# A hybrid encoder on one core: an order of products for each pass, and head products placed side by side in the array

## The chip, the cores and the metric

The kernel runs on one core of one Trainium2 chip. The metric is the device time of one execution, in microseconds; before the change it is 3675.07 us, the median of three runs from 3674.42 to 3675.59. TensorE is called PE (its weight loads PEld), VectorE DVE, ScalarE ACT, GpSimd POOL and SyncE SP.

## The reference

Two layers run over 1024 tokens of 1024 channels. A layer normalises its input, projects it with one wide matrix, runs four token mixers on parts of the projection, gates and projects each mixer's output, adds the four, projects once more and adds the input:

```python
h = _rmsnorm(x, norm_w)
p = h @ w_in
...
u_a = _rwkv7_branch(rw_r, rw_k, rw_v, rw_wlo, rw_alo, rw_z, ...)
u_b = _retention_branch(rt_q, rt_k, rt_v, rt_z, ret_norm_w)
u_c = _ssd_branch(sd_xbc, sd_z, sd_dt, ...)
u_d = _gdn_branch(gd_qkv, gd_z, gd_b, gd_a, ...)
gates = jax.nn.sigmoid(gate_logits.reshape(b, s, N_BRANCH, D_MODEL))
merged = gates[:, :, 0] * (u_a @ w_branch[0])
...
return x + merged @ w_out
```

Retention has 8 heads with 32 channels in q and k and 64 in v; q and k are rotated by a position angle first. RWKV has 8 heads of 64 channels. All is float32. The retention scores, their decay and the state are:

```python
scores = jnp.einsum('bnihk,bnjhk->bnhij', qc, kc) * decay
y_intra = jnp.einsum('bnhij,bnjhv->bnihv', scores, vc)
k_tail = kc * jnp.exp(g_last - g)[..., None]
chunk_state = jnp.einsum('bnjhk,bnjhv->nbhkv', k_tail, vc)
```

## The kernel before

The tokens are cut in two halves of 512, so the program makes four passes: layer 0 on both halves, then layer 1. A pass works on four chunks of 128 tokens.

Most of PE's work is large products: 128 output channels by 512 tokens, summed over 1024 input channels. For float32 accuracy each operand is split in a high and a low part (wh and wl for weights, hH and hL for the normalised input), and three of the four cross products are made, so one such product is 24 matmuls of 128x512. `slab_gemm` (L649) does this; `wide_gemm` (L685) makes the token-major form, in pieces of 128x256; `narrow_gemm` (L669) makes 48 rows of decays. The result stands in one of three PSUM banks called g until DVE or ACT has evacuated it. In the first pass over a layer's weights (passes 0 and 2) ACT casts the high part, DVE subtracts the low part, and both are stored for the second pass (1 and 3), which loads them. SP's queue issues these loads and stores, a fixed number of weight slabs ahead of the product.

The mixers are twelve units a pass: two of retention (four heads each), four of gated delta, two of SSD and four of RWKV (two heads each). Each has a front (scores, triangular inverses) and a back (the state, chunk after chunk), with small products in four PSUM banks called m and one called y. In RWKV's front, `rw_front` (L1501), the low-rank decay and rate are made by two pairs of products (L1514 on), then each chunk's scores for one head after the other: three cross products for each of two operands, 64 rows high, 256 columns wide. In retention's front, `ret_front` (L1724), q is multiplied by four head masks, so that one product of 128 rows by 512 columns gives the scores of four heads; the back (L1768) makes one 128x256 product for the state, masks it, and adds it. `ev_rope` (L884) swaps the two halves of q or k by two copies on ACT.

What sets the order: `FIRST` and `PLAN` (L53, L64) are lists of large products, written by hand, for pass 0 and for the passes after it; an item `in.6.B` is input B of unit 6, `sm` the decays, `merge.ret.3` a gate and a projection, `out.2` an output projection of the pass before, and `norm` starts the normalisation of the next pass. Between the pieces of these products, `mixers` (L1281) puts steps of the mixers: it keeps a reckoning of each engine's time, and a step whose inputs it thinks ready goes next, unless DVE is thought to be more than `LEAD` microseconds behind PE. Each engine then executes its own instructions strictly in the order in which the program was written out.

At the start of the program up to four products run on the input before it is normalised (`h_gemm`, L974; the operands rH and rL lie in tiles called u) and are scaled afterwards. At the end of a pass `norm` makes hH and hL for the next one, which it can do only when the last product that reads the old ones is done.

Of the kernel before, what the change touches and what calls it, by code (L numbers as in the profile page):

```python
# [51 lines left out]

FIRST = items("""  # L53
sm in.0.k in.0.q in.0.v in.0.z0 in.0.z1 in.1.k in.1.q in.1.v in.1.z0 in.1.z1 in.2.v in.2.k in.2.q in.2.z in.3.v
in.3.k in.3.q lora in.3.z in.4.v in.4.k in.4.q merge.ret.0 merge.ret.1 merge.ret.2 merge.ret.3 merge.ret.4 in.4.z
in.5.v in.5.k in.5.q merge.ret.5 in.5.z in.6.x0 in.6.B in.6.C in.6.x1 merge.ret.6 merge.ret.7 in.6.z in.7.x0
in.7.B in.7.C in.7.x1 merge.gdn.0 merge.gdn.1 merge.gdn.2 in.7.z in.8.v in.8.k in.8.r in.8.z in.9.v in.9.k in.9.r
in.9.z merge.gdn.3 merge.gdn.4 in.10.v in.10.k in.10.r merge.gdn.5 merge.gdn.6 merge.gdn.7 merge.ssd.0 in.10.z
merge.ssd.1 in.11.v in.11.k in.11.r merge.ssd.2 merge.ssd.3 merge.ssd.4 in.11.z merge.ssd.5 merge.ssd.6
merge.ssd.7 gate.0 gate.1 gate.2 gate.3 gate.4 gate.5 gate.6 gate.7 norm proj.0 proj.1 proj.2 proj.3 proj.4 proj.5  # L60
proj.6 proj.7
""")

PLAN = items("""  # L64
in.0.k in.0.q in.0.v in.0.z0 in.0.z1 in.1.k in.1.q in.1.v in.1.z0 out.0 sm out.1 out.2 out.3 out.4 out.5 in.1.z1
in.2.v in.2.k in.2.q in.2.z in.3.v in.3.k in.3.q in.3.z in.4.v in.4.k in.4.q out.6 out.7 lora merge.ret.0
merge.ret.1 merge.ret.2 merge.ret.3 in.4.z in.5.v in.5.k in.5.q merge.ret.4 in.5.z in.6.x0 in.6.B in.6.C in.6.x1
merge.ret.5 merge.ret.6 merge.ret.7 in.6.z in.7.x0 in.7.B in.7.C in.7.x1 merge.gdn.0 merge.gdn.1 in.7.z in.8.v
in.8.k in.8.r in.8.z in.9.v in.9.k in.9.r in.9.z merge.gdn.2 merge.gdn.3 in.10.v in.10.k in.10.r merge.gdn.4
merge.gdn.5 merge.gdn.6 merge.gdn.7 merge.ssd.0 in.10.z merge.ssd.1 in.11.v in.11.k in.11.r merge.ssd.2  # L70
merge.ssd.3 merge.ssd.4 in.11.z merge.ssd.5 merge.ssd.6 merge.ssd.7 gate.0 gate.1 gate.2 gate.3 gate.4 gate.5
gate.6 gate.7 norm proj.0 proj.1 proj.2 proj.3 proj.4 proj.5 proj.6 proj.7
""")


def block_cols(kind, idx, role):
    a = np.arange(P)
    if kind == "rw":
        base = {"r": 0, "k": 512, "v": 1024, "z": 1664}[role]
        return base + P * idx + a  # L80
    if kind == "gdn":
        base = {"q": 5256, "k": 5256 + 512, "v": 5256 + 1024, "z": 6792}[role]
        return base + P * idx + a
    if kind == "ret":
        if role in "qk":
            base = 2176 if role == "q" else 2432
            x, h, i = a // 64, (a % 64) // 16, a % 16
# [26 lines left out]
SLABS = [sl for it in PLAN for sl in slabs_of(it)]  # L114
# [4 lines left out]
def sequence(npass):  # L119

    seq = [(p - (it[0] == "out"), it) for p in range(npass) for it in (PLAN if p else FIRST)]
    return [x for x in seq if x != (npass - 1, ("norm",))] + [(npass - 1, it) for it in PLAN if it[0] == "out"]

# [99 lines left out]
def make_consts():  # L223
# [18 lines left out]
    head = (a % 64) // 16  # L242
    put("hmask", (head[:, None] == np.arange(4)[None, :]).astype(f))
# [18 lines left out]
    x = a // 64  # L262
# [8 lines left out]
class Clock:  # L271
# [89 lines left out]
    def ported(self, eng, name, ins):  # L361


        if eng == "scalar" or not ins or any(self.slot.get(x.tensor.name, ("",))[0] in ("m", "g", "y") for x in ins):
            return False
        return eng == "gpsimd" or name in ("tensor_tensor", "scalar_tensor_tensor", "tensor_copy", "copy") \
            or (name == "tensor_scalar" and int(np.prod(ins[0].shape[1:])) >= 32)
# [5 lines left out]
class Engine:  # L373
# [5 lines left out]
    def __getattr__(self, what):  # L379
        fn = getattr(self.real, what)  # L380

        def call(*a, **k):
# [42 lines left out]
class Trunk:  # L425
    LEAD = 3.0
# [44 lines left out]
    def mm(self, out, lhsT, rhs, **k):  # L471
        n, m = (int(np.prod(ap.shape[1:])) for ap in (rhs, lhsT))
# [6 lines left out]
        self.ck.op("pe", [out], [lhsT, rhs], cost)  # L479
# [1021 lines left out]
    def rw_front(self, p, j, inp, box):  # L1501
# [62 lines left out]
        for s in range(2):  # L1564
# [159 lines left out]
    def ret_front(self, p, u, inp, box):  # L1724
# [27 lines left out]
        qms = []  # L1752
        for c in range(NC + 1):
            if c < NC:
                qm = W1(1 + c % 2).rearrange("p (h t) -> p h t", h=4)
# [3 lines left out]
                qms.append(qm)  # L1759
            if c > 0:  # L1760
# [3 lines left out]
            yield  # L1764
# [3 lines left out]
    def ret_back(self, p, u, box):  # L1768
# [6 lines left out]
        yB = self.t([P, 2, 256], "yB")  # L1775
        yC = self.t([P, 2, 256], "yC")
        s16 = self.t([P, NC, 4], "s16")
        for c in range(NC):
            py = self.pm()[:, 0:256]
            self.mm(py, qd[:, c], S, start=True, stop=False, skip_group_check=True)  # L1780
            for h in range(4):
                self.mm(py[:, 64 * h:64 * h + 64], A[:, c, h], va[c // 2][:, c % 2, 64 * h:64 * h + 64],
                                 start=False, stop=(h == 3), skip_group_check=True)
            pst = self.pm()[:, 0:256]
# [312 lines left out]
```

## Time and profile before

| | |
|---|---|
| median of three runs | 3675.07 us |
| the profiled execution's own time | 3677.53 us |
| its span, first to last instruction | 3675.8 us |
| mean granted TensorE clock | 0.981 |
| PE busy | 3535.3 us, 24904 matmuls |
| DVE busy | 2296.0 us |
| ACT busy | 1178.1 us |
| DMA moved | 654.21 MB, mean 178 GB/s |

In the rows of the profile `g<-hL,wh` is an instruction that writes a tile named g from tiles named hL and wh; `128*128 128x512` is the part of the array that it uses, then the size of the moving operand; `x8` is how many there are. A matmul in float32 leaves two records, one whose operands are split beforehand leaves one. A matmul's duration includes its way through the array, so steps are read from start to start. All instructions of DVE, ACT and POOL go through a recording helper and have its line, L400; matmuls have L480, transposes L484. In a row of stretches the columns are the stretch, its length, busy time and count of PE, PEld, DVE, ACT and POOL, the granted clock, the DMA share and GB/s.

### The profile page before, as it was taken

What the parts mean: (1) busy time and instruction counts of PE and PEld (TensorE: products, weight loads), DVE (VectorE), ACT (ScalarE), POOL (GpSimd) and SP (SyncE); (2) the same over time, 40 slices, a digit from 0 to 9 for tenths busy, and PEclk for the clock granted to TensorE, in tenths of its full rate; (3) what the DMA queues carried; (4) which work ended last, traced back from release to release, by engine and by line L of the source; (5) the groups of instructions that cost most, each with busy time, mean ns of one, the idle gap of its engine ahead of it and who ended that gap; (6) DMA issues with size and microseconds to landing.
All of it is one profiled execution on the core that took longest, in us unless ns stands there. A gap on an engine that the chain in (4) does not pass through costs nothing.

```text
span 3675.8 us, 66687 instructions
## 1 busy us (share of the span) xinstructions
PE 3535.3 (96%) x24904; PEld 2855.0 (78%) x24904; DVE 2296.0 (62%) x6038; ACT 1178.1 (32%) x2714; POOL 572.1 (16%) x905
## 2 busy tenths in 40 slices
PE   8998999999999999999999989999999999999998
PEld 6776887777787888777777777877778788877777
DVE  5676767677356655466547676667764666564653
ACT  4333344333132223232224333433331322232221
POOL 2101012221110111122110101122211011112220
PEclk9998999999999999999999999999999999999999
DMA  6573565656665545444676556655566544544356
GB/s 236 174 232 130 196 211 190 200 165 208 210 211 160 150 133 146 134 111 128 199 252 226 185 187 200 208 185 172 185 215 225 177 152 144 149 132 132 104 153 214
DMA packets 359171, 654.21 MB, mean 178 GB/s; under 512 B 39872, under 2 KB 43328, under 8 KB 358848
## 3 DMA queue, kind: packets, MB, share of 16 engines
q1 hardware_dynamic: 347184, 629.92, 54.3%
q10 hardware_dynamic: 11664, 20.02, 1.6%
q8 instruction: 197, 3.23, 0.4%
q14 instruction: 126, 1.03, 0.1%
HBM read 400.23 MB, written 249.56 MB: 177 GB/s over the span
## 4 chain that ended last, share of the span: by engine, by line
PE 83%; DVE 10%; DMA 2%; ACT 2%; issue 1%; POOL 1%; SPq 0%; DVEq 0%; ACTq 0%; POOLq 0%
PE g L480 60%; PE m L480 17%; PE m L484 3%; PE y L480 3%; DVE invw L400 2%; DVE w L400 1%; DMA ws<-wh 1%; DVE wl L400 1%; DVE in L400 1%; DVE cvy L400 1%; DVE yB L400 1%; POOL rs L400 1%; DVE hL L400 0%; ACT w L400 0%; DVE GD L400 0%
## 5 line engine op out<-in xcount | busy, mean ns | idle before, releaser
L480 PE MATMUL g<-hH,wh 128*128 128x512 f32 x2600 | 1075.8, 414 | 0.0
L480 PE MATMUL g<-hL,wh 128*128 128x512 f32 x2600 | 1034.8, 398 | 16.0 <-DVE hL L400 15.9
L480 PE MATMUL g<-hH,wl 128*128 128x512 f32 x2576 | 745.7, 406 | 0.0
L480 PEld LDWEIGHTS g<-hL,wh 128*128 128x128 f32 x2600 | 492.3, 189 | 128.4 <-DVE hL L400 19.3
L480 PEld LDWEIGHTS g<-hH,wh 128*128 128x128 f32 x2600 | 492.0, 189 | 117.5 <-issue 7.1
L480 PEld LDWEIGHTS g<-hH,wl 128*128 128x128 f32 x2576 | 475.7, 190 | 112.1 <-issue 8.1
L480 PE MATMUL g<-u,wh 128*128 128x512 f32 (+1 forms) x1328 | 409.0, 412 | 18.8 <-DVE u L400 11.8
L400 DVE TENSOR_TENSOR wl<-raw,wh 128x512 fp32r<-128x512 f32 x456 | 331.1, 731 | 61.3 <-ACT wh L400 40.3
L400 ACT CAST wh<-raw 128x512 fp32r<-128x512 f32 x447 | 275.2, 619 | 252.5 <-DMA ws<-wh 106.8
L480 PEld LDWEIGHTS g<-u,wh 128*128 128x128 f32 (+1 forms) x1328 | 245.0, 190 | 81.5 <-DVE u L400 18.0
L400 POOL TENSOR_TENSOR rs<-rs,mhalf 128x4 f32<-128x4 f32 (+2 forms) x80 | 106.1, 1327 | 1011.3 <-DVE rs L400 980.4
L400 DVE SCALAR_TENSOR_TENSOR cvy<-cvraw,par,cvy 128x512 f32<-128x512 f32 x244 | 186.5, 764 | 76.8 <-ACT cvy L400 68.3
L480 PE MATMUL g<-u,wl 128*128 128x512 f32 x784 | 223.4, 403 | 0.0
L400 ACT COPY cvraw<-g 128x512 f32<-128x512 f32 (+1 forms) x160 | 93.5, 584 | 301.5 <-PE g L480 254.3
L480 PEld LDWEIGHTS g<-u,wl 128*128 128x128 f32 x784 | 146.3, 190 | 33.3 <-issue 0.5
L400 ACT ACTIVATE tg<-g 128x512 f32<-128x512 f32 x100 | 59.6, 596 | 267.0 <-PE g L480 258.8
L480 PE MATMUL g<-wh,hL 128*128 128x256 f32 x512 | 126.7, 285 | 6.9 <-DVE hL L400 6.9
L480 PE MATMUL g<-wh,hH 128*128 128x256 f32 x512 | 128.4, 288 | 0.0
L400 POOL TENSOR_SCALAR_AFFINE_SELECT GA<-GA 128x512 f32<-128x512 f32 x128 | 86.5, 681 | 249.8 <-ACT GA L400 215.6
L400 POOL TENSOR_TENSOR acc<-acc,tg 128x512 f32<-128x512 f32 x64 | 84.3, 1317 | 241.9 <-DVE tg L400 176.5
L400 ACT ACTIVATE in<-g 128x512 f32<-128x512 f32 x84 | 49.3, 596 | 187.5 <-PE g L480 182.0
L480 PE MATMUL m<-w,w 64*128 64x256 f32 (+1 forms) x640 | 108.3, 299 | 1.0 <-ACT w L400 1.0
(337 smaller groups left out, 5592.8 us busy)
## 6 DMA issues: line engine op xcount, KB each, us to landing
raw<-W SPq DMA_DIRECT2D x456, 256.0 KB, 3.3
ws<-wh SPq DMA_DIRECT2D x456, 256.0 KB, 3.5
ws<-wl SPq DMA_DIRECT2D x456, 256.0 KB, 3.8
wh<-ws SPq DMA_DIRECT2D x456, 256.0 KB, 2.6
wl<-ws SPq DMA_DIRECT2D x456, 256.0 KB, 3.0
w<-x ACTq DMA_DIRECT2D x32, 256.0 KB, 4.2
tg<-rope SPq DMA_DIRECT2D x16, 256.0 KB, 4.3
cvy<-rope SPq DMA_DIRECT2D x16, 256.0 KB, 4.3
```

Of the source, the lines that this page charges most:

```text
L400: return fn(*a, **k)
L480: self.nc.tensor.matmul(out, lhsT, rhs, **k)
L484: self.nc.tensor.transpose(out, in_, ident)
```

## The change

There are seven edits.

- `FIRST` and `PLAN` become `PLANS`, a list for each pass and one for the output products at the end. Within a unit the roles stand in other orders, and large products and merges are mixed otherwise.
- `LEAD` goes from 3 to 20.
- The layout of q and k in retention is head by head (32 rows a head: 16 and 16) instead of half by half, and the swap in `ev_rope` is one shuffle on DVE within 32 rows instead of two copies on ACT.
- RWKV's scores write the two heads in turn, into two banks, so that products on rows 0 to 63 and 64 to 127 follow each other.
- In the low-rank products the two of full height come first, then the two of half height, on different rows.
- Retention's scores are, for each chunk, four products of 32 rows, one for each head, into four banks; there are no masks. The evacuation is four DVE products of 512 columns, as before.
- Retention's state is four products of 32 output rows in one bank, and four updates of 32x64 in place of a masking and an update of 128x256.

```diff
-    LEAD = 3.0
+    LEAD = 20.0
...
-        nc.scalar.copy(sw[0:64], ps[64:128])
-        nc.scalar.copy(sw[64:128], ps[0:64])
+        nc.vector.stream_shuffle(sw, ps, [i ^ 16 for i in range(32)])
...
-        for i, (ps, x) in enumerate(zip((pw, pa), self.lo[l, hf])):
+        xs = list(zip((pw, pa), self.lo[l, hf]))
+        for i, (ps, x) in enumerate(xs):
+            self.mm(ps, up[:, 0, i], x, start=True, stop=False)
+        for i, (ps, x) in enumerate(xs):
             hs = slice(64 * i, 64 * i + 64)
-            self.mm(ps, up[:, 0, i], x, start=True, stop=False)
-            self.mm(ps, up[hs, 1, i], x[hs], start=False, stop=True)
+            self.mm(ps, up[hs, 1, i], x[hs], tiles=2, start=False, stop=True)
...
-                for h in range(2):
-                    hs = slice(64 * h, 64 * h + 64)
-                    pa = self.pm()
-                    for i, pt in enumerate((bp, kp)):
-                        o = pa[:, 256 * i:256 * i + 256]
-                        self.mm(o, pt[hs, 0, cg], ah[hs, c], start=True, stop=False)
-                        self.mm(o, pt[hs, 0, cg], al[hs, c], start=False, stop=False)
-                        self.mm(o, pt[hs, 1, cg], ah[hs, c], start=False, stop=True)
+                pas = [self.pm(), self.pm()]
+                for i, pt in enumerate((bp, kp)):
+                    for n, (x, y) in enumerate(((pt[:, 0], ah), (pt[:, 0], al), (pt[:, 1], ah))):
+                        for h in range(2):
+                            hs = slice(64 * h, 64 * h + 64)
+                            self.mm(pas[h][:, 256 * i:256 * i + 256], x[hs, cg], y[hs, c], tiles=2, start=n == 0,
+                                    stop=n == 2)
+                for h, pa in enumerate(pas):
...
-                for h in range(4):
-                    nc.vector.tensor_scalar(qm[:, h, :], q[:, c * C:c * C + C], self.cc("hmask")[:, h:h + 1], None,
-                                            ALU.mult)
...
-                pa = self.pm()
-                self.mm(pa, k[:, c * C - C:c * C], qms[c - 1].rearrange("p h t -> p (h t)"), start=True, stop=True)
-                nc.vector.tensor_tensor(A[:, c - 1].rearrange("p h t -> p (h t)"), pa, rd, ALU.mult)
...
+        ps = [self.pm() for h in range(4)]
+        for c in range(NC):
+            cs = slice(c * C, c * C + C)
+            for h in range(4):
+                hs = slice(32 * h, 32 * h + 32)
+                self.mm(ps[h][:, cs], k[hs, cs], q[hs, cs], tiles=4, start=True, stop=True)
+        for h in range(4):
+            nc.vector.tensor_tensor(A[:, :, h], c4(ps[h]), rd[:, h * P:h * P + P].unsqueeze(1).to_broadcast([P, NC, C]),
+                                    ALU.mult)
...
-            self.mm(pst, kt[:, c], va[c // 2][:, c % 2], start=True, stop=True)
-            tm, sq = yB[:, c % 2], yC[:, c % 2]
-            nc.vector.tensor_tensor(tm.rearrange("p (h e) -> p h e", h=4), pst.rearrange("p (h e) -> p h e", h=4),
-                                    self.cc("hmask").unsqueeze(2).to_broadcast([P, 4, 64]), ALU.mult)
-            nc.vector.scalar_tensor_tensor(S, S, self.cc("rg")[:, u:u + 1], tm, ALU.mult, ALU.add)
+            for h in range(4):
+                self.mm(pst[H[h]], kt[:, c, H[h]], va[c // 2][:, c % 2, E[h]], start=True, stop=True)
+            for h in range(4):
+                nc.vector.scalar_tensor_tensor(S[H[h], E[h]], S[H[h], E[h]], self.cc("rg")[H[h], u:u + 1], pst[H[h]],
+                                               ALU.mult, ALU.add)
```

The argument `tiles` of `mm` only divides the reckoned cost in the planner. The first items of the lists for pass 0 show the kind of change in the order:

```diff
-sm in.0.k in.0.q in.0.v in.0.z0 in.0.z1 in.1.k in.1.q in.1.v in.1.z0 in.1.z1 in.2.v in.2.k in.2.q in.2.z in.3.v
+in.0.k sm in.0.v in.0.q in.1.k in.0.z0 in.0.z1 in.1.q in.2.q in.1.v lora in.2.v in.1.z0 in.2.k in.3.v in.3.k in.3.q
```

First place: PE in the back of the first retention unit, pass 0. GD, GA, GE, GF and GR are that unit's decayed q, scores, values and decayed k; stret is its state, w the masked q and in the k of the next unit. Before:

```order
L480 MATMUL m_991<-stret_1_95,GD_1_594 128x256
L480 MATMUL m_991<-GE_1_595,GA_2_592 128x64 x4
L480 MATMUL m_997<-GE_1_595,GR_1_593 128x256
L484 MATMUL m_1015<-con_81,in_2_662 128x128 x4
L480 MATMUL m_1021<-stret_1_95,GD_1_594 128x256
L480 MATMUL m_1021<-GE_1_595,GA_2_592 128x64 x4
L480 MATMUL m_1027<-GE_1_595,GR_1_593 128x256
L480 MATMUL m_1041<-stret_1_95,GD_1_594 128x256
L480 MATMUL m_1041<-GF_1_596,GA_2_592 128x64 x4
L480 MATMUL m_1047<-GF_1_596,GR_1_593 128x256
L480 MATMUL m_1059<-w_4_1036,in_2_662 128x512
L480 MATMUL m_1062<-stret_1_95,GD_1_594 128x256
```

And after:

```order
L495 MATMUL m_768<-stret_1_95,GD_1_613 128x256
L495 MATMUL m_768<-GE_1_614,GA_2_611 128x64 x4
L495 MATMUL m_774<-GE_1_614,GR_1_612 32x64 x4
L495 MATMUL g_746<-hH_281,wl_661 128x512 x2
L495 MATMUL g_746<-hH_281,wh_676 128x512
L495 MATMUL g_746<-hL_282,wh_676 128x512
```

Before, one chunk's products follow on the other's with no large product between them; now eight large products stand between the first and the second chunk, of which the first four are shown.

Second place: PE in the backs of gated delta, pass 0. stgdn is the state, b the corrected values, invw and GE belong to the inverse of the next unit. Before:

```order
L480 MATMUL g_3864<-u_2_1087,wl_3793 128x512 x4
L480 MATMUL m_3887<-GA_4_2748,GR_3_2749 128x128
L480 MATMUL m_3887<-stgdn_1_101,GA_4_2748 128x128
L480 MATMUL y_3479<-stgdn_1_101,GA_4_2748 128x128
L480 MATMUL m_3894<-invw_2_3499,GE_3_3453 32x32 x16
L480 MATMUL m_3913<-b_10_3890,GA_4_2748 128x128
L480 MATMUL y_3479<-b_10_3890,GD_3_2750 128x128
L480 MATMUL m_3917<-invw_2_3499 32x32 x16
L480 MATMUL m_3936<-GA_4_2748,GR_3_2749 128x128
```

And after, at a back of the next unit:

```order
L495 MATMUL g_4053<-hH_281,wl_3976 128x512 x2
L495 MATMUL m_4087<-GA_4_3335,GR_3_3336 128x128
L495 MATMUL m_4087<-stgdn_1_102,GA_4_3335 128x128
L495 MATMUL y_4086<-stgdn_1_102,GA_4_3335 128x128
L495 MATMUL g_4053<-hH_281,wl_3976 128x512 x2
L495 MATMUL g_4053<-hH_281,wh_3989 128x512
L495 MATMUL g_4053<-hL_282,wh_3989 128x512
L499 MATMUL m_4104<-con_81,in_7_3684 128x128
```

Before, small products follow on small ones from here until the next large product 27 rows later; now two to six large products stand between the steps of a chunk.

Third place: PE at the end of pass 2. yC is RWKV's last normalised output, on its way to be transposed; nrs belongs to the next pass's normalisation, and the products from u are the last projections. Before:

```order
L480 MATMUL g_28912<-hL_18952,wh_28819 128x512
L484 MATMUL m_29006<-con_81,yC_28829 128x128 x2
L480 MATMUL g_28912<-hH_18951,wl_28855 128x512 x4
L484 MATMUL m_29018<-con_81,nrs_28988 128x128 x4
L480 MATMUL g_29058<-u_8_25952,wh_28866 128x512 x8
```

And after:

```order
L495 MATMUL y_28297<-sa_29037,GA_25_28298 128x64 x2
L495 MATMUL m_29061<-con_81,w_48_28613 128x1 x4
L499 MATMUL m_29069<-con_81,yC_28911 128x128 x2
L499 MATMUL m_29074<-con_81,nrs_29066 128x128 x4
L495 MATMUL g_29114<-u_8_25749,wh_28757 128x512 x8
```

Before, sixteen large products stood between the last product from RWKV's state (`y`) and the projections, twelve of them ahead of these rows and the four with wl within them; now none does.

More of the change, by code (lines that the diff above doesn't have):

```diff
@@ L72 @@
-gate.6 gate.7 norm proj.0 proj.1 proj.2 proj.3 proj.4 proj.5 proj.6 proj.7
-""")
+PLANS = [items(text) for text in ("""
+in.0.k sm in.0.v in.0.q in.1.k in.0.z0 in.0.z1 in.1.q in.2.q in.1.v lora in.2.v in.1.z0 in.2.k in.3.v in.3.k in.3.q
+in.2.z in.1.z1 in.4.k in.3.z in.4.v merge.ret.0 merge.ret.1 in.5.k in.4.q merge.ret.2 merge.ret.3 merge.ret.4 in.5.v
+in.4.z in.5.q in.6.x0 merge.ret.5 in.5.z merge.ret.6 in.6.B in.6.C in.6.x1 merge.ret.7 in.7.B in.7.x0 in.6.z in.7.x1
+merge.gdn.0 in.7.C in.8.v merge.gdn.1 merge.gdn.2 in.7.z in.8.k in.8.r in.9.v in.8.z in.9.k merge.gdn.3 in.9.r
@@ new lines @@
+merge.gdn.4 merge.gdn.5 merge.gdn.6 in.10.v in.9.z merge.gdn.7 in.10.k in.10.r merge.ssd.0 in.11.v in.10.z
+merge.ssd.1 merge.ssd.2 merge.ssd.3 merge.ssd.4 merge.ssd.5 in.11.r in.11.k merge.ssd.6 merge.ssd.7 gate.0 gate.1
+in.11.z gate.2 gate.3 gate.4 gate.5 gate.6 gate.7 proj.0 proj.1 norm proj.2 proj.3 proj.4 proj.5 proj.6 proj.7
+""", """
+in.0.k in.0.q in.1.k in.1.q out.0 in.0.v out.1 out.2 out.3 in.0.z1 sm in.0.z0 in.1.v out.4 out.5 in.2.v in.1.z0
+in.2.q in.3.v in.2.k in.3.k in.3.q in.2.z out.6 in.1.z1 out.7 in.4.q in.4.k in.4.v lora merge.ret.0 in.3.z
@@ new lines @@
+proj.1 proj.2 proj.3 proj.4 proj.5 proj.6 gate.7 norm proj.7
+""", """
+in.0.q sm in.0.v in.0.z0 in.0.k in.0.z1 in.1.k in.1.q in.1.v out.0 in.2.v in.2.k in.3.v in.3.k in.1.z1 out.1 out.2
+in.2.q out.3 in.1.z0 in.2.z out.4 out.5 in.3.q in.3.z in.4.v in.4.k out.6 out.7 lora merge.ret.0 in.4.q merge.ret.1
+merge.ret.2 merge.ret.3 in.5.q in.4.z in.5.v in.5.k merge.ret.4 in.6.C in.6.B merge.ret.5 in.5.z in.6.x1 in.6.x0
+in.7.B merge.ret.6 merge.ret.7 in.6.z in.7.x0 merge.gdn.0 merge.gdn.1 in.7.x1 in.8.r in.7.C in.7.z in.8.v in.8.k
@@ new lines @@
+merge.gdn.2 in.9.r in.8.z merge.gdn.3 in.9.v in.9.z merge.gdn.4 merge.gdn.5 merge.gdn.6 merge.gdn.7 in.9.k in.10.k
+in.10.r merge.ssd.0 in.10.v in.10.z merge.ssd.1 in.11.k in.11.v in.11.r merge.ssd.2 merge.ssd.3 merge.ssd.4
+merge.ssd.5 merge.ssd.6 merge.ssd.7 in.11.z gate.0 gate.1 gate.2 gate.3 gate.4 gate.5 gate.6 gate.7 norm proj.0
+proj.1 proj.2 proj.3 proj.4 proj.5 proj.6 proj.7
+""", """
+in.0.q in.0.z1 in.0.k in.0.v in.0.z0 in.1.q in.1.k in.1.z0 out.0 sm out.1 in.1.v out.2 out.3 in.2.k out.4 out.5
@@ L76, in block_cols @@
+merge.ssd.5 in.11.k in.11.z merge.ssd.6 merge.ssd.7 gate.0 gate.1 gate.2 gate.3 gate.4 gate.5 gate.6 gate.7 norm
+proj.0 proj.1 proj.2 proj.3 proj.4 proj.5 proj.6 proj.7
+""", """
+out.0 out.1 out.2 out.3 out.4 out.5 out.6 out.7
+""")]
 def block_cols(kind, idx, role):
@@ L111, in slabs_of @@
     return {"gate": [("gate", b, it[-1], 0), ("gate", b, it[-1], 1)], "proj": [("proj", b, it[-1])], "norm": []}[it[0]]
-SLABS = [sl for it in PLAN for sl in slabs_of(it)]
+SLABS = [sl for it in PLANS[1] for sl in slabs_of(it)]
 NSLAB = len(SLABS)
@@ L119, in sequence @@
 def sequence(npass):
-    seq = [(p - (it[0] == "out"), it) for p in range(npass) for it in (PLAN if p else FIRST)]
-    return [x for x in seq if x != (npass - 1, ("norm",))] + [(npass - 1, it) for it in PLAN if it[0] == "out"]
+    return [(p - (it[0] == "out"), it) for p in range(npass + 1) for it in PLANS[p] if (p, it) != (npass - 1, ("norm",))]
 def pack_weights(w_in, w_branch, w_out):
@@ L241, in make_consts @@
         put(f"l{b}", ((a[:, None] % 32 // b % 2 == 1) & (a[:, None] % 32 // b == c // b + 1)).astype(f))
-    head = (a % 64) // 16
-    put("hmask", (head[:, None] == np.arange(4)[None, :]).astype(f))
+    head = a // 32
     rd = np.zeros((2, P, 6, P), f)
@@ L261, in make_consts @@
     i16 = a % 16
-    x = a // 64
+    x = a % 32 // 16
     ct = cos[:, i16].T
@@ L366, in ported @@
         return eng == "gpsimd" or name in ("tensor_tensor", "scalar_tensor_tensor", "tensor_copy", "copy") \
-            or (name == "tensor_scalar" and int(np.prod(ins[0].shape[1:])) >= 32)
+            or (name == "tensor_scalar" and int(math.prod(ins[0].shape[1:])) >= 32)
     def free(self, eng, port=False):
@@ L385, in call @@
             outs = [out] + ([k["accum_out"]] if k.get("accum_out") is not None else [])
-            n = max(int(np.prod(x.shape[1:])) for x in ops)
+            n = max(int(math.prod(x.shape[1:])) for x in ops)
             if what == "dma_start":
-                self.clock.transfer(self.name, a[0], a[1], int(np.prod(a[0].shape)) / 256)
+                self.clock.transfer(self.name, a[0], a[1], int(math.prod(a[0].shape)) / 256)
             else:
@@ L468, in cc, with mm @@
         return self.con[:, c - P:c - P + w]
-    def mm(self, out, lhsT, rhs, **k):
-        n, m = (int(np.prod(ap.shape[1:])) for ap in (rhs, lhsT))
+    def mm(self, out, lhsT, rhs, tiles=1, **k):
+        n, m = (int(math.prod(ap.shape[1:])) for ap in (rhs, lhsT))
         if rhs.dtype != F32:
@@ L478, in mm @@
             cost = 2 * max(n, m) * 0.85e-3
-        self.ck.op("pe", [out], [lhsT, rhs], cost)
+        self.ck.op("pe", [out], [lhsT, rhs], cost / tiles)
         self.nc.tensor.matmul(out, lhsT, rhs, **k)
```

45 lines of the change are left out of this document (17 added, 28 removed).

## The prediction

> **What bounds the kernel now.** I read the page's busy rows first, then the stretches with their granted clock, then who PE waits for.
>
> ```profile
> PE 3535.3 (96%) x24904; PEld 2855.0 (78%) x24904; DVE 2296.0 (62%) x6038; ACT 1178.1 (32%) x2714; POOL 572.1 (16%) x905
> PE 83%; DVE 10%; DMA 2%; ACT 2%; issue 1%; POOL 1%; SPq 0%; DVEq 0%; ACTq 0%; POOLq 0%
> PE g L480 <- DVE hL L400: 22.8, 6, 7.2
> PE m L480 <- DVE invw L400: 18.7, 19, 4.3
> PE m L480 <- DVE GR L400: 18.2, 5, 6.1
> ```
>
> The reader is to see that TensorE is the bound (96% of 3675.8 us, 83% of the chain that ended last), and that its idle time, 140 us, is nearly all waiting for DVE. So a product taken off PE is worth its step, and a filled wait its length, unless DVE ends last there. The waits are not spread evenly:
>
> ```profile
> 60.00:931.00 871.00, 822.09 (x5870) 663.48 (x5869) 607.92 (x1548) 331.39 (x759) 138.22 (x224) 0.97 0.59 194
> 1813.00:2741.00 928.00, 886.48 (x6224) 717.25 (x6224) 631.31 (x1602) 343.27 (x781) 144.54 (x229) 0.97 0.62 203
> 104.00:130.00 26.00, 17.36 (x68) 12.01 (x67) 13.86 (x38) 4.67 (x12) 4.18 (x2) 0.78 0.17 60
> 286.00:352.00 66.00, 51.35 (x318) 42.48 (x319) 45.98 (x134) 21.66 (x60) 8.25 (x12) 0.81 0.40 132
> 2076.00:2154.00 78.00, 60.98 (x497) 50.62 (x496) 54.33 (x159) 23.72 (x64) 9.59 (x17) 0.88 0.42 138
> sum 170.00, PE 129.69 PEld 105.11 DVE 114.16 ACT 50.06 POOL 22.02; mean PE 43.23 PEld 35.04 DVE 38.05 ACT 16.69 POOL 7.34
> ```
>
> The last four rows are one answer: three short stretches, of passes 0 and 2, in which few large products stand between the small ones. PE idles 170.0 - 129.7 = 40.3 us of them, and the granted clock falls to 0.78, 0.81 and 0.88. A timeline shows how it looks there (start, duration, and in brackets the wait):
>
> ```profile
> 53.13 0.58 PE L480 MATMUL g<-wh,hL 128*128 128x256 f32 x1 [5.03 <-DVE hL L400]
> ...
> 111.49 1.12 PE L480 MATMUL m<-stret,GD 128*128 128x256 f32 x2 [2.83 <-DVE stret L400]
> 126.52 1.12 PE L484 MATMUL m<-con,GA 128*128 128x128 f32 x4 [3.75 <-DVE GA L400]
> ...
> 329.90 0.60 PE L484 MATMUL m<-con,in 128*128 128x128 f32 x4
> 338.88 0.65 PE L480 MATMUL m<-invw,GE 32*32 32x32 f32 x32 [3.79 <-DVE invw L400]
> 349.72 1.08 PE L484 MATMUL m<-con,yB 128*128 128x128 f32 x4 [2.62 <-DVE yB L400]
> ```
>
> The first row is the program's start, where the first wide product (in chunks of 128x256) has caught up with hL, the low half of the normalised input, which DVE still makes. The others lie in the first two stretches. After a wait four 128x128 transposes take 1.08 us instead of 0.60: a wait costs clock as well as its own length.
>
> **The change, part by part.** All is worked from the profiled execution, 3677.5 us, 2.5 us above the median of the three runs, 3675.07.
>
> RWKV scores: 64 groups of twelve 64-row products, six per head. One group, between large ones:
>
> ```profile
> 769.09 0.40 PE L480 MATMUL g<-hH,wh 128*128 128x512 f32 x1
> 769.32 0.39 PE L480 MATMUL g<-hL,wh 128*128 128x512 f32 x1
> 769.64 0.38 PE L480 MATMUL m<-w,w 64*128 64x256 f32 x1
> 769.87 0.28 PE L480 MATMUL m<-GE,w 64*128 64x256 f32 x1
> 769.99 0.40 PE L480 MATMUL m<-w,w 64*128 64x256 f32 x3
> 770.21 0.28 PE L480 MATMUL m<-GE,w 64*128 64x256 f32 x2
> 770.33 0.39 PE L480 MATMUL m<-w,w 64*128 64x256 f32 x3
> 770.56 0.28 PE L480 MATMUL m<-GE,w 64*128 64x256 f32 x1
> 770.68 0.28 PE L480 MATMUL m<-w,w 64*128 64x256 f32 x1
> 770.89 0.45 PE L480 MATMUL m<-invw 32*32 32x32 f32 x32
> 771.27 0.50 PE L480 MATMUL g<-hH,wh 128*128 128x512 f32 x1
> ```
>
> A large product steps 0.23 us, a score 0.12 (769.87 to 769.99). Written order is w, GE, w, w, GE, w for a head, then the same for the other; the rows, which stand in order of start, instead show three, two and three together, and an x3 that ends within 0.40 although one lasts 0.28 and the next alone starts 0.12 later. So the second head's first products already run beside the first head's last: the eleven steps take 770.68 - 769.64 = 1.04, not 0.23 + 10 x 0.115 = 1.38. Three of six overlap; the change writes the heads in turn, so that all six can. Six pairs take 0.23 + 4 x 0.115 = 0.69, saving 0.35 x 64 = **22 us**. Bounds: 0, if no more overlap is to be had, and 40 (half of a whole 1.25 us, 769.64 to 770.89, times 64).
>
> "TensorE: Matmul & The Clock Gate" of the Trainium skill, Part 3, says that matmuls are "strict FIFO, no reordering". This trace does not agree: by that rule the written order would show, and the term would be 64 x (1.38 - 0.69) = 44 us, an estimate.
>
> The 32x32 products show four tiles side by side: 32 in 771.27 - 770.89 = 0.38. They also price a change of tile form, about 0.1 us at either end.
>
> Lora, retention scores, retention states:
>
> ```profile
> 2342.16 1.01 PE L480 MATMUL m<-lo,w 128*128 128x512 f32 x2
> 2343.10 0.93 PE L480 MATMUL m<-la,w 128*128 128x512 f32 x2
> 1000.36 0.86 PE m L480 x2
> 2341.86 0.65 PE L480 MATMUL m<-GF,GR 128*128 128x256 f32 x2
> 2434.82 0.34 PE L480 MATMUL m<-GF,GE 128*64 128x64 f32 x4
> 2434.99 0.29 PE L480 MATMUL m<-sa,GE 128*64 128x64 f32 x4
> 2435.21 0.66 PE L480 MATMUL y<-sa,GA 128*128 128x64 f32 x4
> ```
>
> Lora: each of four steps about 0.43; two half-height ones side by side save 0.43 x 16 units = **7 us** (bounds 0, 7). Retention scores: 32 products of 0.86 (third row, from the chain) are 27.5 us. They become 128 products, 256 records, of 32 rows by 128 columns. Alone each would step like a full 128x128, (0.60 - 0.27)/3 = 0.11: 28 us, no gain. Four side by side: 7 us, and 8 x 0.3 for changes of form: 9.5, saving **18 us** (bounds 0, 20.5); I take this end because the 32x32 rows do so. Retention states: a product of 256 columns is half of the one of 512, 0.43; it becomes four products, eight records, in 32-column tiles. The nearest, eight records in 64-column tiles, take 2435.21 - 2434.82 = 0.39. 32 of these save **1 us**, between 10 saved (a quarter of the time, as for the scores) and 6 lost (two changes of form, 32 x 0.2).
>
> "TensorEngine Tiling (Array Packing)" of the Trainium skill, Tiling Modes, says that a change of mode drains the array; it gives no price. By it the states' term would be about nothing, which lies in these bounds.
>
> DVE:
>
> ```profile
> L400 DVE TENSOR_SCALAR w<-in,con 128x128 f32<-128x128 f32 x128 | 27.4, 280 | 0.0
> L400 DVE TENSOR_TENSOR yB<-m,con 128x256 f32<-128x256 f32 x32 | 13.6, 424 | 48.1 <-PE m L480 48.1
> L400 DVE SCALAR_TENSOR_TENSOR stret<-stret,con,yB 128x256 f32<-128x256 f32 x32 | 15.6, 486 | 1.2
> L400 DVE SCALAR_TENSOR_TENSOR sh<-m,fc,sf 64x64 f32<-64x64 f32 x96 | 27.1, 282 | 37.2 <-POOL sh L400 21.4 <-PE m L480 14.5
> L400 DVE TENSOR_TENSOR in<-g,tg 128x512 f32<-128x512 f32 x14 | 9.7, 692 | 45.6 <-ACT cvraw L400 43.9 <-DMA tg<-rope 1.8
> ```
>
> Gone are 27.4 + 13.6 + 15.6 = 56.6 us; new are 128 state updates like sh, 128 x 0.28 = 36, and 16 shuffles like the 128x512 row, 11 (the shuffle is in no row: 0 to 23, twice that). Net 10 less (0 to 20). ACT loses two half copies per q and k. PE hides all of it except in the first stretch above, so it is not a term. A state's chain of four updates is 1.13 against 0.91, 0.2 us later; large products now stand behind it. The new wait: the score step takes all four m banks at once, and the next small product on PE, of whichever mixer, waits until DVE has evacuated one, at worst all four, 4 x 0.69 = 2.8 us; behind the first of these steps stand fourteen large products in PE's order, 14 x 0.23 = 3.2, so I cost it at nothing. Uncovered it would be 8 x 2.8 = 22.
>
> Order: in the three stretches the row lists above put large products between the small ones. I take 0.8 of 40.3 idle, 32 us, and of the lost clock (0.22 x 26 + 0.19 x 66 + 0.12 x 78 = 28) 16. At the start the wide product now runs on the unnormalised input, before hL exists, in the place of one normal product: 24 more large steps, 5.6 us, stand ahead of the wait of 5.03: 5. Together **53 us** (bounds: 0, where each wait only moves, and 91: all of the stretches' 40.3 and 28 and all of hL's 22.8). At the ends of the passes DVE has the same normalisation and evacuations to make before PE can go on, so those hL waits stay; the end of pass 2 loses the sixteen large products that stood between the last RWKV state and the first projection, 16 x 0.23 = 3.7 us, of which I charge 3, since the transpositions still lie between. The program has 825 groups of small products between large ones instead of 752: 73 x 0.1 = 7. New short waits elsewhere: 7, my choice, a twentieth of 140. Net 36. The weight loads and the copies of the split weights move with their products on SP's queue, as do the rotary tables, so queue and bytes stay as they are; the DMA share of 0.59 and 0.62 in the two split passes leaves room, and I cost them at nothing. Were one slab late, it would be a landing, some 3 us, once.
>
> Sum: 22 + 7 + 18 + 1 + 36 = 84. 3677.5 - 84 - 2.5 = **3591 us**.
>
> **The rivals.** *Waits only move*: DVE is 0.70 and 0.68 busy in the two split passes, so its queue may hand each filled wait on; only the 48 us of array work stay, 3677.5 - 48 - 2.5 = 3627. For it: PE's waits are for DVE in nearly every row. Against it: DVE's busy time in the three stretches, 114.2 of 170.0, is no larger a share than in the whole pass, so there it is chains, not a full engine, that PE waits for. *Order pays in full*: 91 for 53, 3591 - 38 = 3553; against it, hL's rows at the ends of passes. *Tiles do not run side by side*: the row tiles serialise, 36 stays, 3677.5 - 36 - 2.5 = 3639; against it, the x3 rows. *Slower, by LEAD*: the planner lets mixers run while DVE is 20 us behind (was 3). A product's evacuation then can stand behind 20 us of DVE work; three g banks cover two products, 2 x 24 x 0.23 = 11. From 11 us of backlog PE stops, up to 9 us each. Once in each of 12 units of passes 0 and 2 is 24 x 9 = 216, 3591 + 216 = 3807; in half of them 3699, slower than before, and the point from which it is slower is ten of them. Against it: DVE today waits for PE's products, not they for it.
>
> **How the numbers follow.** Forecast 0.52, waits move 0.20, full pay 0.14, no side by side 0.08, LEAD 0.06. A measurement can tell 0.2%, 7 us, from no change. Faster 0.90 (all but LEAD, less 0.04 for the edge of waits that move and no side by side together), same 0.04, slower 0.06. Range 3540 to 3648: it takes in all rivals but LEAD; below 3540 the bounds of scores and order would have to hold together.
>
> **What would show it.** Right: score groups of 0.9 us; retention scores near 1.2 us per unit; the stretches' clock at 0.95 or more and PE's idle below 110. Wrong: score groups still at 1.25; PE's wait for hL, GR or u longer in total; waits of large products on g banks (DVE in, tg), which today are none.

## The result, and the profile after

The changed kernel takes **3520.64 us** (median of 4 runs, 3520.22 to 3521.93), the kernel before beside it 3675.33: a ratio of 0.9577, with a 95% interval of 0.9560 to 0.9593. That is 155 us less, where 84 were forecast; it lies below the range. The profiled execution has a span of 3518.3 us, 157.5 less than before's 3675.8.

The page's busy rows, its chain by engine, and the main rows of PE's waits (in total, how often, the longest), of the changed kernel:

```profile
PE 3449.7 (98%) x25288; PEld 2793.3 (79%) x25288; DVE 2292.2 (65%) x6018; ACT 1152.2 (33%) x2671; POOL 585.4 (17%) x905
PE 88%; DVE 7%; DMA 2%; issue 1%; ACT 1%; POOL 0%; SPq 0%; DVEq 0%; ACTq 0%; POOLq 0%
PE m L495 <- DVE invw L414: 21.6, 13, 13.9
PE g L495 <- ACT u L414: 6.4, 1, 6.4
PE g L495 <- DVE in L414: 6.2, 5, 4.6
PE g L495 <- DVE acc L414: 4.9, 1, 4.9
PE g L495 <- DVE hL L414: 4.4, 3, 4.0
PE g L495 <- DVE cvy L414: 1.5, 1, 1.5
PE g L495 <- DVE cvraw L414: 0.9, 1, 0.9
```

PE idles 3518.3 - 3449.7 = 68.6 us, where it idled 140.5. The waits for hL fell from 22.8 to 4.4; those for GR (18.2) are in no row any more. The rows in, acc, cvy and cvraw are new: each of these 13.5 us ended with a DVE instruction that reads a bank g, so large products wait for their banks here, which they did not before. DVE is as busy as before, 2292 us against 2296, so PE does not wait less because DVE has less to do.

The second gain is the clock. A view of stretches (PE and the other engines busy, then the granted clock, DMA share and rate) of the two passes whose rows the prediction shows:

```profile
60.00:884.00 824.00, 801.13 (x6002) 647.23 (x6000) 602.84 (x1545) 325.12 (x752) 150.66 (x230) 0.99 0.62 206
1729.00:2590.00 861.00, 852.58 (x6275) 691.43 (x6276) 618.71 (x1584) 332.33 (x764) 150.69 (x229) 0.99 0.65 215
```

It was 0.97 in both. The trace tells when the clock is granted at half: before, 22 times, 140.7 us of the span, during 98.3 of which PE worked. Work at half clock takes about twice its time (four products with wl take 2.36 us at half clock, 1.08 otherwise; both stand in rows further down), so 98.3 / 2 = 49.2 us were lost. After, it is 7 times, 58.9 us, 35.0 of them with work: 17.5 us lost. So every span splits into three parts: PE's idle time, the half clock's loss, and the rest, which is PE's work at full clock. Before 140.5 + 49.2 + 3486.1; after 68.6 + 17.5 + 3432.2. Of the 157.5 us, **72 are idle time, 32 clock and 54 work**.

The work's 54 are nearly all the array's. The timeline of one group of RWKV's scores, after:

```profile
756.86 0.40 PE L495 MATMUL g<-hL,wh 128*128 128x512 f32 x1
757.19 0.39 PE L495 MATMUL m<-w,w 64*128 64x256 f32 x2
757.41 0.28 PE L495 MATMUL m<-GE,w 64*128 64x256 f32 x2
757.52 0.40 PE L495 MATMUL m<-w,w 64*128 64x256 f32 x4
757.75 0.29 PE L495 MATMUL m<-GE,w 64*128 64x256 f32 x2
757.87 0.29 PE L495 MATMUL m<-w,w 64*128 64x256 f32 x2
758.09 0.50 PE L495 MATMUL g<-hH,wh 128*128 128x512 f32 x1
758.43 0.39 PE L495 MATMUL g<-hL,wh 128*128 128x512 f32 x1
```

Every product now has its partner: the steps take 757.87 - 757.19 = 0.68 us (0.69 was worked out), and from the first score to the next large product it is 0.90, as forecast. What a group costs is read from the large product ahead of it to the second one behind, less two large steps, because the one right behind starts slowly too: here 1.57 - 0.47 = 1.10. Over all groups that stand alone the median went from 1.454 to 1.106: 64 x 0.348 = 22.3 us. One retention unit's scores, of before (one of four products) and of the changed kernel (all):

```profile
999.97 0.40 PE L480 MATMUL g<-acc,wh 128*128 128x512 f32 x1
1000.20 1.02 PE L480 MATMUL m<-w,in 128*128 128x512 f32 x2
1000.66 0.80 PE L480 MATMUL g<-u,wh 128*128 128x512 f32 x1
1001.29 0.39 PE L480 MATMUL g<-acc,wh 128*128 128x512 f32 x1
```

```profile
965.60 1.08 PE L495 MATMUL g<-u,wl 128*128 128x512 f32 x4
966.61 1.17 PE L495 MATMUL m<-in,in 32*128 32x128 f32 x32
967.71 0.50 PE L495 MATMUL g<-u,wh 128*128 128x512 f32 x1
968.05 0.40 PE L495 MATMUL g<-acc,wh 128*128 128x512 f32 x1
```

Before, 1001.29 - 999.97 - 0.47 = 0.85 for each of 32 (median 0.857): 27.4 us. After, from the last of the four records with wl, at 966.29, to 968.05, less 0.47: 1.30 for each of 8 units, 10.4. Saved: 17.0.

### The profile page after: what moved, and what is told of

It reads as the page before. It is cut to its first block, busy times and chain, and to the rows that moved or that the text cites. A ratio compares the mean times of both kernels' runs of the same rounds, so it can differ in the third digit from the quotient of the medians.

```text
span 3518.3 us, 67362 instructions
## 1 busy us (share of the span) xinstructions
PE 3449.7 (98%) x25288; PEld 2793.3 (79%) x25288; DVE 2292.2 (65%) x6018; ACT 1152.2 (33%) x2671; POOL 585.4 (17%) x905
## 4 chain that ended last, share of the span: by engine, by line
PE 88%; DVE 7%; DMA 2%; issue 1%; ACT 1%; POOL 0%; SPq 0%; DVEq 0%; ACTq 0%; POOLq 0%
PE g L495 66%; PE m L495 16%; PE m L499 3%; PE y L495 3%; DVE invw L414 2%; DVE w L414 1%; DVE wl L414 1%; DVE in L414 1%; DMA ws<-wl 0%; DVE hL L414 0%; DVE cvy L414 0%; ACT u L414 0%; POOL rs L414 0%; DVE acc L414 0%; DMA wh<-ws 0%
## 5 line engine op out<-in xcount | busy, mean ns | idle before, releaser
L495 PE MATMUL g<-hH,wh 128*128 128x512 f32 (+1 forms) x2608 | 1074.6, 412 | 6.3 <-DVE acc L414 4.9
L495 PE MATMUL g<-hL,wh 128*128 128x512 f32 (+1 forms) x2608 | 1031.4, 395 | 4.5 <-DVE hL L414 4.4
L495 PEld LDWEIGHTS g<-hH,wh 128*128 128x128 f32 (+1 forms) x2608 | 491.4, 188 | 120.9 <-issue 7.1
L495 PEld LDWEIGHTS g<-hL,wh 128*128 128x128 f32 (+1 forms) x2608 | 492.2, 189 | 104.9 <-DVE hL L414 7.2
L495 PE MATMUL g<-u,wh 128*128 128x512 f32 (+1 forms) x1312 | 397.2, 409 | 18.8 <-ACT u L414 6.4
L414 ACT COPY cvraw<-g 128x512 f32<-128x512 f32 x132 | 77.4, 586 | 265.8 <-PE g L495 237.3
L414 ACT ACTIVATE tg<-g 128x512 f32<-128x512 f32 x100 | 59.7, 597 | 211.2 <-PE g L495 203.7
L495 PE MATMUL g<-wh,hH 128*128 128x256 f32 x480 | 119.8, 287 | 0.0
L495 PE MATMUL g<-wh,hL 128*128 128x256 f32 x480 | 117.4, 282 | 0.0
L414 DVE TENSOR_TENSOR invw<-m,invw 128x4 f32<-128x4 f32 (+3 forms) x480 | 87.0, 181 | 23.3 <-PE m L495 8.4
```

The lines of the kernel that those rows point to most:

```text
L414: return fn(*a, **k)
L495: self.nc.tensor.matmul(out, lhsT, rhs, **k)
```

## The experiments

**The parts apart and together.** The change has three: the array edits (with the unmasked retention and the shuffle), the new lists of items, and LEAD 20. All eight combinations are measured. Going from the changed kernel back to the old lists and LEAD 3 changes these lines, where FIRST and PLAN are the texts of before:

```
-PLANS = [items(text) for text in (...)]
+PLANS = [FIRST, PLAN, PLAN, PLAN, [("out", n) for n in range(8)]]
-    LEAD = 20.0
+    LEAD = 3.0
```

The array edits alone:

> The changed kernel with the old lists of items (one list for pass 0, one for all later passes) and LEAD 3: the array edits, the shuffle and the unmasked retention alone. Theory A (the shortfall of the prediction is the order's): about 45 us below the kernel before, 3630, as the trace of after has 64 x 0.35 = 22 us less for RWKV's scores, about 15 less for retention's scores and 8 less for lora; PE's waits stay near 125 us. Theory B (the array edits and the masks taken from DVE shorten the waits too): 80 us or more, 3595 or less, with PE's waits below 100 us.

The lists and LEAD 20 alone:

> The kernel before with the new lists and LEAD 20, and none of the array edits (masks, two copies and heads one after the other as before). Theory A: 155 - 45 = 110 us below before, 3565, with PE's waits near 60 us and a clock of 0.99. Theory B (the new lists are fitted to the lighter DVE and need the array edits): 70 us or less, 3605 or more, with waits of 90 us or more.

All but LEAD:

> The changed kernel with LEAD 3 instead of 20. If the lists carry the order's gain: within 15 us of 3520. If LEAD carries it (mixers may run ahead of DVE, so their steps stand between large products): 40 us or more above, 3560. If the 13.9 us wait of pass 0 is the price of the backlog that LEAD 20 allows, that wait is gone here.

All but the lists:

> The changed kernel with the old lists and LEAD 20. If the lists carry the order's gain: like array_only, about 3630. If LEAD carries it: about 3530 to 3560. The prediction's rival of a slower kernel by LEAD would show here as waits of large products for their banks (PE g waiting for DVE in, tg or cvraw) of more than 30 us.

LEAD alone, and the lists alone:

> The kernel before with LEAD 20, old lists, no array edit. Theory A (each part is worth the same wherever it stands): LEAD gave 39 us beside the array edits (3662 to 3623), so 3636 here. Theory C (LEAD sets how long small products stand without a large one between them; the waits move to the large products, whose banks and inputs come later, unless the lists are made for it): 3640 to 3660, stretches over 4 us without a large product down from 157 us to about 70, waits ahead of large products up from 42 to 55 us or more.

> The kernel before with the new lists alone: LEAD 3, no array edit. Theory A: the lists gave 44 us beside the array edits at LEAD 3, so 3631 here. Theory C: the lists fit LEAD 20, so the waits of small products stay: 3630 to 3660, with more than 150 us in stretches over 4 us without a large product.

Median times, and each profiled span split as above (us). The last column adds up the stretches without large products, each from the start of the first small product to the start of the next large one, where this is over 4 us:

| | array edits | lists | LEAD | time | ratio to before (95%) | idle | half clock | work | without large |
|---|---|---|---|---|---|---|---|---|---|
| before | no | old | 3 | 3675.1 | | 140.5 | 49.2 | 3486.1 | 157 |
| array_only | yes | old | 3 | 3662.4 | 0.9961 (0.9947 to 0.9975) | 159.9 | 59.7 | 3439.4 | 170 |
| lead20_before | no | old | 20 | 3658.9 | 0.9951 (0.9933 to 0.9969) | 124.0 | 41.9 | 3492.2 | 116 |
| lists_before | no | new | 3 | 3644.3 | 0.9915 (0.9900 to 0.9930) | 126.0 | 38.2 | 3479.4 | 151 |
| plans_old | yes | old | 20 | 3623.3 | 0.9856 (0.9842 to 0.9871) | 135.5 | 51.9 | 3434.8 | 71 |
| lead3 | yes | new | 3 | 3618.3 | 0.9844 (0.9829 to 0.9859) | 134.0 | 56.5 | 3424.3 | 196 |
| order_only | no | new | 20 | 3607.1 | 0.9814 (0.9799 to 0.9828) | 93.8 | 30.5 | 3482.3 | 70 |
| after | yes | new | 20 | 3520.6 | 0.9577 (0.9560 to 0.9593) | 68.6 | 17.5 | 3432.2 | 44 |

Three things stand in it. *Work* depends on the array edits alone: 3479 to 3492 without, 3424 to 3439 with. *LEAD* shortens the stretches without large products, from 151 to 196 us down to 44 to 116. The likely reason stands in the code of `mixers`: with 3, steps of the mixers stop as soon as the planner's DVE is more than 3 us behind its PE, large products are used up in the meantime, and the chains run bare later. The parts *do not add*: alone they bring 13, 16 and 31 us, 60 in all, together 155. In each of the three old or half-old orders the array edits save 47 to 57 us of work and lose 21 to 30 of it to idle time and half clock; with the new lists and LEAD 20 they save 50 and win 38 more. So lists and LEAD together bring 68 by themselves (order_only), the array edits 13, and 74 come only from having both. Theory A missed both of its first runs (3630 and 3565 for 3662 and 3607) and, with 3636 and 3631, the last two; B had order_only but not array_only: the edits shorten no wait by themselves. C's times hold for the last two, though lead20_before keeps more bare stretches (116 us) than it put, and its waits ahead of large products rose from 42 to 46 us, not to 55. lead3 and plans_old fit neither single cause: taking back LEAD alone loses 98 us, taking back the lists alone 103. The 13.9 us wait of pass 0 is no price of LEAD 20: at LEAD 3 it lasts 14.1.

Where the waits go in plans_old (same columns as above):

```profile
PE m L478 <- DVE invw L397: 32.1, 23, 3.7
PE m L482 <- DVE yB L397: 13.2, 7, 4.6
PE g L478 <- DVE cvy L397: 12.1, 3, 6.1
PE g L478 <- DVE wl L397: 8.2, 7, 2.8
PE g L478 <- DVE cvraw L397: 7.5, 4, 3.7
```

The rows for cvy and cvraw are large products (g) that wait for a bank until DVE has evacuated it, but for 3.7 us of cvraw's that end with a memset: this is the mechanism of the rival "slower, by LEAD". (The row for wl is another thing: the low half of a weight that DVE makes late.) Counted over all rows, the waits that end with an instruction of DVE reading a bank g come to 0 to 0.8 us in the four runs with LEAD 3, and with LEAD 20 to 18.5 here, 16.4 in lead20_before, 19.2 in order_only and 13.5 after. So LEAD 20 brings them with the old lists and with the new, and they are far from the 108 to 216 that the rival was priced at. The waits for hL go the other way, also by LEAD: 17.8 to 28.0 us with 3, 3.5 to 4.8 with 20.

**Products put in another order, with nothing else moved.** In these three kernels the planner saw what it saw before, so every other instruction stands where it stood. RWKV's scores in turn, in the kernel before:

```
+                        for h in range(2):
...
+                            self.nc.tensor.matmul(pas[h][:, 256 * i:256 * i + 256], x[hs, cg], y[hs, c], ...)
```

> The kernel before with only the products of RWKV's scores written in turn for the two heads; every other instruction on every engine stays where it was. Theory A (PE's own time is what falls, whatever the order): 64 x 0.35 = 22 us less, 3653. Theory B (in the old order PE runs up against DVE's chains, so that part of a saving comes back as a wait): 5 to 15 us less, 3660 to 3670, with PE's waits longer by the rest. A strict queue without overlap before: 44 us less, 3631.

And one head after the other, in the changed kernel:

```
...
+                                    stop=n == 2, late=late[h])
+                for out, lhsT, rhs, kw in late[0] + late[1]:
+                    self.nc.tensor.matmul(out, lhsT, rhs, **kw)
```

> The changed kernel with RWKV's scores of one head after the other again, and every other instruction where it is. Theory A: 64 x 0.35 = 22 us more, 3543. Theory B for the new order (waits are filled, so PE's time counts whole): also 22, against less than that in the old order; the difference between this run's loss and the gain of heads_in_before is what the order does to a saving.

In the changed kernel it costs 3542.67 - 3520.64 = 22.0 us: theory A, and the 22 of the prediction. In the kernel before the profiled span falls by 21.9 us, 24.6 of work less and 2.8 of idle time more; the runs, whose times spread over 9 us, give 14.6 (ratio 0.9959, 0.9946 to 0.9971). How much of the 22 the old order takes back lies between 2 and 11, then, and is not settled. The strict queue (44) is excluded by both.

Retention's scores, head after head in the changed kernel:

```
             for h in range(4):
...
-                self.mm(ps[h][:, cs], k[hs, cs], q[hs, cs], tiles=4, start=True, stop=True)
+                self.mm(ps[h][:, cs], k[hs, cs], q[hs, cs], tiles=4, start=True, stop=True, late=late[h])
+        for out, lhsT, rhs, kw in sum(late, []):
+            self.nc.tensor.matmul(out, lhsT, rhs, **kw)
```

> The changed kernel with retention's 128 score products written head after head (four of the same rows in a row, then the next four) in place of the four heads in turn; nothing else moved. If tiles of different rows run side by side only when they follow each other: the 256 records go from 9 us to about 25, 16 us more, 3537. If the array takes them as they come ready whatever the written order: within 3 us of 3520.

It takes 3534.10, 13.5 us more. The unit's timeline:

```profile
971.03 1.08 PE L498 MATMUL g<-u,wl 128*128 128x512 f32 x4
972.04 2.82 PE L1780 MATMUL m<-in,in 32*128 32x128 f32 x32
974.79 0.50 PE L498 MATMUL g<-u,wh 128*128 128x512 f32 x1
975.12 0.40 PE L498 MATMUL g<-acc,wh 128*128 128x512 f32 x1
```

The same 32 records take 2.75 us instead of 1.10 (972.04 to 974.79, against 966.61 to 967.71). Products of the same rows run one behind the other; those of other rows share the array with them only over a short reach. By the starts of the records, at each of the three changes of rows three records run beside the last three of the block before, and all others step alone by 0.11 us. At 2.94 for a unit, 23.5 us for all, the smaller products in the old manner of writing would have saved 4 us, not 17.

**What a wait does to the clock.** In the kernel before, 20 useless transposes ahead of one product in each pass:

```
+        if base == 16:
+            self.cnt["inv16"] = self.cnt.get("inv16", 0) + 1
+            if self.cnt["inv16"] % 4 == 1:
+                for _ in range(20):
+                    self.nc.tensor.transpose(pb[:, 0:P], self.cc("ident"), self.cc("ident"))
```

> The kernel before with 20 useless transposes (128x128, whose result the next product overwrites) ahead of the first 128x480 product of each pass, where PE waited 6.1, 3.3, 4.2 and 3.3 us for GR. They fill 2.2 us of each wait. Theory: a wait costs its length and then half the clock for 3.4 or 6.8 us, in 3.41 us pieces, once it is longer than some 2.3 to 3 us; so three of these four waits (about 1.1, 2.0 and 1.1 us left) bring no half clock, and the two 128x480 records with the four products behind them take 1.7 us less each there: about 6 us less, 3669. Rival (the clock falls with the kind of small product that runs, not with the wait): the half clock stays and the time is the same or longer.

It takes 3668.85 us, 5.2 less (ratio 0.9986, 0.9977 to 0.9995): more work, and a shorter time. The place in pass 1, of before and with the transposes:

```profile
1108.42 0.39 PE L480 MATMUL g<-hL,wh 128*128 128x512 f32 x1
1112.15 1.97 PE L480 MATMUL m<-GR,con 128*128 128x480 f32 x2 [3.34 <-DVE GR L400]
1113.19 2.36 PE L480 MATMUL g<-hH,wl 128*128 128x512 f32 x4
1115.39 0.39 PE L480 MATMUL g<-hH,wh 128*128 128x512 f32 x1
```

```profile
1104.65 2.35 PE L1405 MATMUL m<-con 128*128 128x128 f32 x20
1108.15 1.07 PE L480 MATMUL m<-GR,con 128*128 128x480 f32 x2 [1.16 <-DVE GR L400]
1108.69 1.47 PE L480 MATMUL g<-hH,wl 128*128 128x512 f32 x4
1109.99 0.40 PE L480 MATMUL g<-hH,wh 128*128 128x512 f32 x1
```

GR comes no earlier. But after a wait of 1.16 us the six records take 1.84 us, after one of 3.34 they take 3.24. The same place as stretches, of before and with the transposes; the granted clock is the third number from the end:

```profile
1108.50:1111.70 3.20, 0.31 (x2) 0.00 (x0) 3.09 (x12) 0.00 (x0) 0.00 (x0) 0.99 0.30 87
1111.70:1115.10 3.40, 2.95 (x5) 1.83 (x6) 2.14 (x12) 0.00 (x0) 0.00 (x0) 0.50 0.00 0
1115.10:1119.00 3.90, 3.90 (x18) 3.12 (x18) 3.32 (x18) 0.56 (x2) 0.00 (x0) 1.00 0.56 154
```

```profile
1108.10:1111.50 3.40, 3.35 (x13) 2.47 (x14) 2.83 (x15) 0.00 (x0) 0.00 (x0) 1.00 0.08 5
```

Three of the four half-clock stretches at these places are gone (the fourth wait still lasts 3.94 us), and over the whole span 49.2 us lost have become 43.0. So at these three places it is the wait that costs the clock, not the kind of product behind it.

**By degrees, and how fine the fit is.** `LEAD = 5.0` in the changed kernel:

> The changed kernel with LEAD 5. At 10 the planner writes exactly the order that it writes at 20. If LEAD's gain comes by degrees: between 3618 (LEAD 3) and 3520, about 3550, with 60 to 130 us in stretches over 4 us without a large product. If it is a matter of all or nothing: 3520 to 3530 or 3600 and more.

3579.36 us (0.9741, 0.9726 to 0.9756): by degrees, with 101 us in bare stretches. (At LEAD 10 the planner writes the same order on PE as at 20; on DVE and ACT a few lines differ.) Then the planner's costs alone, and two items of one list:

```
-        self.ck.op("pe", [out], [lhsT, rhs], cost / tiles)
+        self.ck.op("pe", [out], [lhsT, rhs], cost)
```

> The changed kernel with one number of the planner undone: it counts products in row tiles at their full cost again (cost instead of cost / tiles). Every product and its form stay; only the order that the planner writes differs (2080 lines on PE, 985 on DVE). PE's own work should stay at 3432 us. If the lists fit the one order that the planner writes with these costs (theory C): idle and half clock go from 86 us to 110 or more, 3545 to 3590. If the lists are good for any order near it, so that the array edits' own time makes the difference: within 10 us of 3520.

> The changed kernel with two neighbouring items of pass 1's list exchanged (in.3.v in.2.k becomes in.2.k in.3.v), which moves 328 lines on PE. If the fit is as fine as single items: 5 to 25 us more than 3520. If only the broad shape of the lists counts: within 5 us.

With the old costs it takes 3543.86 (0.9643, 0.9629 to 0.9657), 23 more; work is 3434, idle time 87.6 instead of 68.6. Idle time and half clock come to 106 us, just under the 110 that theory C put. So the same products with the same durations lose 23 us by the written order alone: the lists suit the order that the planner writes from these costs. Single items matter less: the exchange gives 3521.87, no difference. The three parts bring 155 - 60 = 95 us only together; that the 23 belong to these, and that the rest has the same cause, is argued, not shown.

**One wait filled.** The longest wait left, 13.9 us for invw near 185 us, with one step put off:

```
+            if self.cnt["inv16"] == 1:
+                self.ck.step += 12.0
```

> The changed kernel with one step put off: after the first gated-delta unit's solving on DVE the planner counts 12 us more, so that large products are written ahead of the 32x32 products that waited 13.9 us near 185 us. If the wait is only a place in the order: the 13.9 us and the half clock of 17 us go, 10 to 17 us less than 3520, 3503 to 3510. If the gated-delta chain is the bound of pass 0 there: the wait comes back within the next 150 us and the time stays within 5 us of 3520.

3516.72 us (3511.93 to 3518.32), 4 us less. Beside the kernel before, the ratio is 0.9567 (0.9552 to 0.9582), which overlaps with that of the changed kernel, so a gain is not shown; the time is what was expected if the chain of gated delta is the bound there. Its timeline:

```profile
175.27 0.60 PE L499 MATMUL m<-con,in 128*128 128x128 f32 x4
183.88 1.09 PE L499 MATMUL m<-con,in 128*128 128x128 f32 x4 [8.01 <-DVE invw L414]
```

Other small products now stand first and wait for the same solving on DVE (probably for an m bank that it still reads): 8.0 of the 13.9 us come back. The half clock there falls from 17.1 to 10.2 us, but two new stretches of 3.4 stand elsewhere, and PE loses 17.9 us by it in all, as before (17.5).

## Why the prediction was wrong

**The array's terms were right.** RWKV's scores: 22 forecast, 22.3 by the groups, 22.0 by undoing them. Retention's scores: 18, against 17.0. Lora: 7, against 9.8 (a group with the same 12 small records around it takes 3.470 before and 2.862 in array_only, the median of four; 0.61 x 16). That is above the bound of 7; the sum left out that the old order changed form four times in a group and the new does twice, which at 0.1 each would be about 3 us, an estimate from the prediction's own price. Retention's states: 1, against 1.4 (1.755 to 1.712 for a chunk). Together 48, against 50.5. "Tiles do not run side by side" (3639) is excluded by them. The rule "strict FIFO, no reordering" of "TensorE: Matmul & The Clock Gate" of the Trainium skill, Part 3, would have made the first term 44; neither run that changes only this order bears it out. But these are sums of PE's work: in the old order 30 of 47 us came back as waits and half clock (array_only), so that they count in full only with the new one.

**DVE was right in the main.** Its busy time fell by 4 us where 10 were worked out (0 to 20); the updates of the state cost 35.5 us in place of 36, the shuffle 11.8 in place of 11. The score step's four m banks brought no wait that any row shows, as was costed.

**The order's term was wrong: 36 forecast, 107 measured** (157.5 - 50.5: 72 idle, 32 clock, 3 other). Of the 107, 69 are the new order's own (order_only, by its span); the other 38 of idle time and half clock appear only when the array edits stand in that order. The sum had no place for these, since it added each part as if it stood alone, and why they come is not shown beyond the planner's costs above. Three choices made the term small.
- It took waits from three stretches (32 us) and from the program's start (5), for which it had rows of the new order, and let all others stand. But the order was rewritten everywhere. At the place in pass 1 above, 8 large products stood between the last m<-w,w (128x256) and the 128x480 product, with a wait of 3.34; after, 22 stand there and nothing waits. The waits for hL at the ends of passes were held to be DVE's own chain that stays; LEAD 20 alone takes them from 22.8 to 3.5, with 16.4 us of new waits for banks beside it.
- It took 16 us of clock from the three stretches, where the whole loss, 49.2 us, comes in 22 stretches, most of them right at a long wait. "TensorE: Matmul & The Clock Gate", Part 1, tells of an activity window of about 3.4 us that runs on its own; the trace agrees, with pieces of 3.41 us. A long wait has a price of its own besides its length, then, and the half-clock stretches of before could have been counted one by one, as above.
- It charged 17 us for more changes of form, new short waits and the end of pass 2. With both lists and LEAD work did not rise (order_only has 3482.3, before 3486.1), and at the end of pass 2 the wait of 3.8 us for hL is gone and the longest one left is 1.5.

**The rivals.** "Order pays in full" (3553) was the nearest, and still 32 us too high, since its 91 us were those of the same places. "Slower, by LEAD" had its mechanism right (its sign, large products waiting for g banks, is there with 13.5 us) and its size some ten times too large; what it left out is that without LEAD 20 98 of the 155 us are gone (3618), as 103 are without the lists (3623). "Waits only move" is what the array edits do alone: 47 us of work saved, 13 of time.

## What to carry to other kernels

Split the span into idle time, half clock and work before pricing a change: here the three parts answer to different edits, and the first two were 190 of 3676 us, of which 104 are gone. Where a change writes a new order everywhere, count what stands ahead of each long wait in the new order, not at two or three places. And measure the parts of such a change together with the order made for them: alone, the edits that shorten the bound engine's work gave back up to two thirds of it.

## What the hardware showed beyond that

The half clock comes in pieces of 3.41 us (3.41, 6.83, 10.24, and so on up to 23.9), whatever the wait's length; only the last stretch of each run is cut off by the end. No one length decides: of waits of PE that stand alone, one of 3.34 us (array_only, at 1109.5) was followed by no half clock, and one of 1.24 us among small products (plans_old, at 3339.7) was. The same page of the Trainium skill, "TensorE: Matmul & The Clock Gate", asks for no idle gaps above about 3.4 us (HAM oscillation); seven of before's 22 half-clock stretches stand at waits of 2.0 to 3.34 us, with no longer one beside them.

Products of different row tiles share the array over a short reach in the written order. Where they stand in turn, 32 records take 1.10 us; in blocks of eight records of the same rows they take 2.75, and only three records at each change of rows run beside the block before. RWKV's scores show the same reach: three of six pairs overlap where one head stands after the other. So PE's rows, which stand in order of start, are not strictly in the written order there.
